# A bidirectional mixer layer on one core: the triangular substitution moved from VectorE to GpSimd, with its transposes placed later

## The chip, the cores and the metric

The kernel runs on 1 core of one Trainium2 chip. The metric is the time on the device of one execution, in microseconds. Before the change three runs took 2184.51, 2187.23 and 2191.09 us, with a median of 2187.23 us.

The engines go by their names in the profile: PE is TensorE (PEld its loading of weights), DVE is VectorE, ACT is ScalarE, POOL is GpSimd, SP is SyncE, which issues the DMAs here. Each engine works through its own queue in order and waits for others by semaphores.

## The reference, cut to what matters

The reference is one encoder layer over a sequence of 1024 positions with 1024 channels. A normalised, modulated input h is projected by w_in to all branches; three branches mix along the sequence (A an mLSTM, B a long convolution, C the RWKV-7 recurrence); their gated outputs are merged and projected. The change lies in branch C, which runs this recurrence in both directions for 16 heads of 64 channels:

```python
def rwkv7_scan(r, w, k, v, kk, a, reverse):
    def step(state, inp):
        r_t, w_t, k_t, v_t, kk_t, a_t = inp
        sa = jnp.einsum('bhij,bhj->bhi', state, -kk_t)
        state = (state * w_t[:, :, None, :] + sa[..., None] * (kk_t * a_t)[:, :, None, :]
                 + v_t[..., None] * k_t[:, :, None, :])
        return state, jnp.einsum('bhij,bhj->bhi', state, r_t)
    xs = tuple(jnp.moveaxis(t.astype(jnp.float32), 1, 0) for t in (r, w, k, v, kk, a))
    _, ys = lax.scan(step, jnp.zeros((B, H, N, N), jnp.float32), xs, reverse=reverse)
    return jnp.moveaxis(ys, 0, 1)
...
proj = h @ w_in[l]
```

The kernel computes it in chunks of 64 positions. Within a chunk each sa depends on those before it, which is a triangular system of 64 x 64 for each head, direction and chunk. The kernel inverts these systems ahead of the scan.

## The kernel before

**Stages.** The kernel normalises the input and forms h (`modulate`), runs branches A and B, then branch C (`rwkv`), then the merge. Beside the branches it works off a list of jobs, which are projections of h by tiles of w_in. One job's tile of weights is loaded in four parts (`load_w`): ScalarE rounds a part to wh (L333), GpSimd makes the rest wl = wraw - wh (L334), and TensorE multiplies three times per 128 channels (L351 to L353). There are four buffers of wh and of wl, as many as one tile has parts, so a part of the next tile is made only when TensorE is through with the same part of the tile before.

**Branch C.** `rwkv` goes over 8 pairs of heads. The scan of a pair (`scan`) has 16 chunks m, each with four yields, so 64 steps. One chunk is a chain: TensorE forms U, VectorE copies it to us (L1769), TensorE multiplies us by the inverse tt to SA, VectorE and ScalarE copy SA into SV (L1775, L1776), TensorE forms SN, VectorE adds the state and scales it (sn, L476), and VectorE and ScalarE copy the result into SV for the next chunk (L1800, L1801). `setup` makes G and B for two chunks at a time.

**What runs beside the scan.** `weave` runs the scan and, at fixed steps, the next piece of other generators: `prep` (the factors ar and bk of a half pair), `load`, `bonus` and `post` (the head's norm and output), and `tphase`. Between the steps it works off the projections (`fill`). The inverses come from `tphase`, in two groups: those of chunks 8 to 15 of a pair (g = 1) while chunks 1 to 6 are scanned, those of chunks 0 to 7 of the next pair (g = 0) while chunks 10 to 15 are scanned. The step tuples of `put` say at which of the 64 steps each piece is issued. The pieces of `tphase` are issued under `ahead(..., TP)`, which raises their priority by 400 instructions.

**One tphase.** TensorE forms the products pq, ScalarE copies them out to quad and q21, VectorE transposes quad into Ab (L1625), and a DMA fills Tb with its initial value (L1628). Then the substitution runs over 31 rows: row l forms a product tm of column l of Ab with row l of Tb (L1633) and adds it into the rows of Tb below (L1636), 62 instructions in all, each dependent on the one before. Both are issued by the helper `tt`, so the profile files them under its line, L476. The rows are issued in pieces of five. Then two transposes on VectorE make t1 (L1641) and t2 (L1644), TensorE multiplies q21 by t1 to pw, ScalarE copies that to W and t2 into tt, TensorE multiplies W by t2 to px, and ScalarE copies px into tt.

**The order on an engine.** A scheduler puts each engine's instructions in order by priority, ahead of the run. `issue_after(x)` lets an instruction come no earlier in that order than x, and `in_turn` keeps groups of products together. On the chip each engine keeps to its order.

Of the kernel before, what the change touches and what calls it, by code (L numbers as in the profile page):

```python
# [23 lines left out]
TP, PP, PW, RA = 400, 0, 3, 2  # L24
# [4 lines left out]
MUL, ADD, SUB, MAX, MIN = ALU.mult, ALU.add, ALU.subtract, ALU.max, ALU.min  # L29
# [16 lines left out]
def run(g):  # L46
    for _ in g:
        pass
# [11 lines left out]
def ahead(tc, gen, by):  # L60

    while True:
        if by:
            with tc.high_priority(by):
                if next(gen, gen) is gen:
                    return
        elif next(gen, gen) is gen:
                return
        yield


def weave(fg, at, fill, per):

    i, owed = 0, 0.0
    for _ in fg:
        for g in at.pop(i, ()):
            next(g, None)
        owed += per
        fill(int(owed))
        owed -= int(owed)  # L80
        i += 1
    for i in sorted(at):
        for g in at[i]:
            next(g, None)
# [201 lines left out]
class Trunk:  # L286
# [1060 lines left out]
    def rwkv(self, yc_out, pairs=range(8)):  # L1347
        nc, tc, A = self.nc, self.tc, self.A
        with ExitStack() as c2:
# [37 lines left out]

            pairs = list(pairs)
            n = len(pairs)
            cx = [dict(p=p, ar={}, al={}, bk={}, pc={}) for p in pairs]  # L1390
            run(self.load(cx[0]))
            for g in range(2):
# [8 lines left out]
            for i in range(n):  # L1401
                at = {}

                def put(gen, *steps):
                    for s in steps:
                        at.setdefault(s, []).append(gen)
                put(prep1, 0, 0, 1, 2, 3, 4, 4)
                put(self.bonus(cx[i]), 5, 6, 7)
                put(ahead(tc, self.tphase(cx[i], 1), TP), *range(6, 28, 2))
                if i + 1 < n:  # L1410
                    nx = cx[i + 1]
                    put(self.load(nx, cx[i - 1] if i else None), 8, 9, 10, 11)
                    put(ahead(tc, self.prep(nx, 0, 0), PP), 15, 16, 19, 33, 33)
                    put(ahead(tc, self.prep(nx, 0, 1), PP), 34, 35, 36, 37, 37)
                    put(ahead(tc, self.tphase(nx, 0), TP), *range(39, 62, 2))
                    prep1 = ahead(tc, chain(self.prep(nx, 1, 0), self.prep(nx, 1, 1)), PP)
                    put(prep1, 40, 42, 49)
                if i > 0:
                    put(self.post(cx[i - 1], yc_out, i + 1 == n), 5, 6, 7, 8, 11, 12, 13, 14)
                weave(self.scan(cx[i], cx[i + 1] if i + 1 < n else None), at, self.fill, max(0, self.left() - 6) / (64.0 * (n - i + 0.1)))  # L1420
# [176 lines left out]
    def tphase(self, cx, g):  # L1597

        nc, rp = self.nc, self.rp
        x2 = lambda n: self.ep.tile([128, 16, 32], F32, name=n, tag="x2", bufs=3)
        q, q21 = x2("quad"), self.ep.tile([128, 16, 32], F32, name="q21", tag="q21", bufs=1)
        pq = [x.rearrange("p (c t) -> p c t", t=CL) for x in self.banks("pq")]
# [19 lines left out]
        Ab = self.ep.tile([128, 32, 32], F32, name="Ab", tag="Ab", bufs=1)  # L1624
        nc.vector.transpose(Ab.rearrange("p t (g u) -> p t g u", g=2),  # L1625
                            q.rearrange("p u t -> p t u").unsqueeze(2).broadcast_to([128, 32, 2, 16]))
        Tb = x2("Tb").rearrange("p a b -> p (a b)").rearrange("p (t s) -> p t s", s=16)
        nc.sync.dma_start(Tb, self.A["tinit"])  # L1628
        tm = rp.tile([128, 136], F32, name="tm", tag="tm", bufs=1)
        for l in range(31):  # L1630
            n, m = 31 - l, l // 2 + 1
            x = tm[:, 0:n * m].rearrange("p (a b) -> p a b", b=m)
            self.tt(x, Ab[:, l + 1:32, l].unsqueeze(2).broadcast_to([128, n, m]),  # L1633
                    Tb[:, l, 0:m].unsqueeze(1).broadcast_to([128, n, m]))
            o = Tb[:, l + 1:32, 0:m]
            self.tt(o, o, x, ADD)  # L1636
            if l % 5 == 4:
                yield
        tt = self.tt_t[g]
        t1 = x2("t1").rearrange("p a b -> p (a b)").rearrange("p (v s) -> p v s", s=16)  # L1640
        nc.vector.transpose(t1.rearrange("p v s -> p s v"), Tb.rearrange("p t s -> p s t"))  # L1641
        t1 = t1.rearrange("p (g u) s -> p u s g", g=2)
        t2 = x2("t2")
        nc.vector.transpose(t2.rearrange("p u (s g) -> p u s g", g=2), t1)  # L1644
# [95 lines left out]
    def scan(self, cx, nx):  # L1740

        nc, rp = self.nc, self.rp
# [11 lines left out]
        for m in range(16):  # L1754
# [4 lines left out]
            if j == 0:  # L1759
                ahead = self.setup(cx, m // 2 + 1) if m < 14 else self.setup(nx, 0) if nx else iter(())  # L1760
            ch = self.ps.tile([128, 4, 2, CL], F32, name="pch", tag="c", bufs=2)
            U, SA, SN, py = (ch[:, i] for i in range(4))
# [3 lines left out]
            if late:  # L1766
                late[0](ins)
            us = self.sm.tile([128, 2, CL], F32, name="us", tag="us", bufs=2)
            nc.vector.tensor_copy(us, U)  # L1769
            ins = self.in_turn(partial(nc.tensor.matmul, SA[hsl[h], d], tt[hsl[h], 8 * d + c, :], us[hsl[h], d],  # L1770
                                       start=True, stop=True) for d in range(2) for h in range(2))
            if late:
# [143 lines left out]
```

## Time and profile before

| | before |
|---|---|
| median of 3 runs | 2187.23 us |
| lowest, highest | 2184.51, 2191.09 us |
| profiled execution, own time | 2200.05 us |
| its span (first to last instruction) | 2198.3 us |
| mean granted TensorE clock | 0.956 |
| first to last copy of us (the scan stage) | 929.5 to 1983.3 us |

The profile is of one execution, which has its own time. A row of the groups of instructions gives the line, the engine, the operation, what it writes and reads, the shapes and how often, then the busy time in all and the mean of one, then the idle time ahead of them and what ended it. A row of the timeline gives the start and the length in us. A row of windows gives a stretch, its length, the busy time of each engine with its count of instructions, the granted clock and the DMA share. A row of the waits names who waited for whom, the sum, the count and the longest. TensorE's matmuls are pipelined, so its busy time contains more than the time in which its array computes.

### The profile page before, as it was taken

To read this page: it belongs to the slowest core of one execution; us is meant where nothing else is said; L and a number is where in the kernel's file an instruction comes from. 1 tells how busy PE (TensorE), PEld (TensorE's weight loads), DVE (VectorE), ACT (ScalarE), POOL (GpSimd) and SP (SyncE) were. 2 spreads that over 40 slices of the span, in tenths; PEclk is the share of its full clock that TensorE was granted. 3 is DMA by queue.
4 is the path that set the end of the run, shared out by engine and by line. 5 is a ranking of instruction groups with operands and counts; after the bars stand their busy time and mean duration, and the time that the engine had idled before them with its cause. 6 is when DMAs were issued, how large, how long until landed. Compare 5 with 4: busy or idle time off the path is not lost. (4 is left out here: it accounts for less than half of the span.)

```text
span 2198.3 us, 45984 instructions
## 1 busy us (share of the span) xinstructions
PE 1994.0 (91%) x17098; PEld 1509.2 (69%) x17098; DVE 1634.6 (74%) x4754; ACT 1103.2 (50%) x2558; POOL 424.3 (19%) x485
## 2 busy tenths in 40 slices
PE   6999899999989899899989999999898887897998
PEld 4666777787868677666766676666666665675786
DVE  4854999988447947788787888868887888764536
ACT  5557356454242115664665756667466564532221
POOL 2211311122222432311101111111114411010200
PEclk9999999999999999999998999999899998897999
DMA  8211222334465345321322333224143542445623
GB/s 255 70 67 59 78 77 90 112 101 127 143 200 172 119 138 163 124 68 61 130 79 93 117 106 102 92 81 136 52 155 118 187 144 63 159 143 175 196 89 129
DMA packets 169384, 262.19 MB, mean 119 GB/s; under 512 B 17863, under 2 KB 87335, under 8 KB 169160
## 3 DMA queue, kind: packets, MB, share of 16 engines
q1 hardware_dynamic: 169160, 259.25, 36.3%
q8 instruction: 135, 2.21, 0.4%
q14 instruction: 89, 0.73, 0.1%
HBM read 181.06 MB, written 78.12 MB: 118 GB/s over the span
## 5 line engine op out<-in xcount | busy, mean ns | idle before, releaser
L334 POOL TENSOR_TENSOR wl<-wraw,wh 128x256 fp32r<-128x256 f32 x408 | 371.5, 915 | 1488.6 <-ACT wh L333 1464.8
L351 PE MATMUL pg<-hh,wh 128*128 128x512 f32 x1440 | 601.5, 418 | 20.9 <-ACT wh L333 11.8
L352 PE MATMUL pg<-hh,wl 128*128 128x512 f32 x1440 | 594.3, 413 | 16.4 <-POOL wl L334 16.3
L353 PE MATMUL pg<-hl,wh 128*128 128x512 f32 x1440 | 592.4, 412 | 1.9 <-DVE hl L565 1.8
L351 PEld LDWEIGHTS pg<-hh,wh 128*128 128x128 f32 x1440 | 278.7, 194 | 88.9 <-ACT wh L333 15.1
L352 PEld LDWEIGHTS pg<-hh,wl 128*128 128x128 f32 x1440 | 279.3, 194 | 78.0 <-POOL wl L334 22.2
L353 PEld LDWEIGHTS pg<-hl,wh 128*128 128x128 f32 x1440 | 278.1, 193 | 62.0 <-DVE hl L565 2.8
L333 ACT CAST wh<-wraw 128x256 fp32r<-128x256 f32 x408 | 162.7, 404 | 220.6 <-PE pg L353 122.1
L476 DVE TENSOR_TENSOR tm<-Ab,Tb 128x126 f32<-128x126 f32 (+22 forms) x496 | 145.4, 293 | 4.4 <-DMA Tb<-in_tinit 2.7
L476 DVE TENSOR_TENSOR Tb<-Tb,tm 128x126 f32<-128x126 f32 (+22 forms) x496 | 144.2, 291 | 1.9
L473 DVE SCALAR_TENSOR_TENSOR st<-pg,hmu,st 128x511 f32<-128x511 f32 (+1 forms) x130 | 80.9, 636 | 27.9 <-ACT e L424 17.6
L476 DVE TENSOR_TENSOR G<-pgr,gmask 128x512 f32<-128x512 f32 x128 | 85.4, 679 | 17.0 <-PE pgr L398 17.0
L457 ACT ACTIVATE st<-pg 128x512 f32<-128x512 f32 x74 | 44.2, 597 | 99.9 <-PE pg L353 95.0
L1684 ACT COPY G<-ar 64x128 f32<-64x128 f32 x256 | 64.3, 295 | 48.4 <-DVE G L476 46.6
L473 DVE SCALAR_TENSOR_TENSOR st<-st,pg 128x512 f32<-128x512 f32 x80 | 54.3, 679 | 35.7 <-PE pg L353 12.7
L398 PE MATMUL pgr<-ar,bk 64*128 64x128 f32 x896 | 76.9, 287 | 0.0
L141 DVE SCALAR_TENSOR_TENSOR row<-row 64x1 f32<-64x1 f32 x393 | 72.7, 208 | 2.1
L1769 DVE COPY us<-pch 128x128 f32<-128x128 f32 x128 | 36.3, 283 | 45.8 <-PE pch L398 45.5
L395 PEld LDWEIGHTS pch<-SV,G 128*64 128x64 f32 x256 | 25.3, 139 | 65.5 <-ACT SV L1801 52.3
L395 PE MATMUL pch<-SV,G 128*64 128x64 f32 x256 | 43.2, 252 | 27.7 <-ACT SV L1801 26.2
L476 DVE TENSOR_TENSOR dw<-dw,dw 128x512 f32<-128x512 f32 x92 | 67.1, 760 | 0.9
L395 PEld LDWEIGHTS pch<-SV,B 128*64 128x64 f32 x256 | 25.3, 139 | 60.1 <-ACT SV L1776 50.1
(677 smaller groups left out, 4228.4 us busy)
## 6 DMA issues: line engine op xcount, KB each, us to landing
wraw<-in_w_in SPq DMA_DIRECT2D x340, 128.0 KB, 2.3
low<-lora SPq DMA_DIRECT2D x32, 512.0 KB, 4.1
sig<-st SPq DMA_DIRECT2D x48, 256.0 KB, 2.6
st<-sig SPq DMA_DIRECT2D x48, 256.0 KB, 3.5
wraw<-in_w_br SPq DMA_DIRECT2D x68, 128.0 KB, 2.8
adw<-in_ada_w SPq DMA_DIRECT2D x16, 512.0 KB, 7.1
x<-in_x SPq DMA_DIRECT2D x8, 512.0 KB, 6.1
hx<-st SPq DMA_DIRECT2D x16, 256.0 KB, 2.0
```

The costliest lines, as they stand in the source:

```text
L141: self.ops.append(lambda: self.nc.vector.scalar_tensor_tensor(o, a, s, b, op0=op0, op1=op1))
L333: self.nc.scalar.copy(hi, raw)
L334: self.nc.gpsimd.tensor_tensor(lo, raw, hi.bitcast(F32), op=SUB)
L351: nc.tensor.matmul(p, wh, hh, start=(k == 0), stop=False)
L352: nc.tensor.matmul(p, wl, hh, start=False, stop=False)
L353: nc.tensor.matmul(p, wh, hl, start=False, stop=(k == n - 1))
L395: ins = f()
L398: ins = f()
L457: self.nc.scalar.activation(o, p, AF.Tanh, scale=0.5)
L473: return self.nc.vector.scalar_tensor_tensor(out, in0, s, in1, op0=op0, op1=op1)
L476: return self.nc.vector.tensor_tensor(out, a, b, op=op)
L1684: nc.scalar.copy(G[0:64, :, d, h, 0:64], cx["al"][g, d, b % 4][hsl[h]])
```

## The change

The 62 instructions of a substitution are issued on GpSimd instead of VectorE. The scan notes its latest copy of us in `self.mark`, and the first transpose (t1) may stand in VectorE's order no earlier than the one that is latest when it is issued. `tphase` has one more yield, between the substitution and the transposes, and the steps at which its pieces are issued change: the substitution's pieces now follow at consecutive steps, and the transposes stand at steps 24 and 57 (before at 20 and 53), the parts behind them at 26, 28 and 59, 61 (before at 22, 24 and 55, 57).

```diff
+            self.mark = None
...
-                put(ahead(tc, self.tphase(cx[i], 1), TP), *range(6, 28, 2))
+                put(ahead(tc, self.tphase(cx[i], 1), TP), 6, *range(7, 14), 24, 26, 28)
...
-                    put(ahead(tc, self.tphase(nx, 0), TP), *range(39, 62, 2))
+                    put(ahead(tc, self.tphase(nx, 0), TP), 39, *range(40, 47), 57, 59, 61)
...
         for l in range(31):
             n, m = 31 - l, l // 2 + 1
             x = tm[:, 0:n * m].rearrange("p (a b) -> p a b", b=m)
-            self.tt(x, Ab[:, l + 1:32, l].unsqueeze(2).broadcast_to([128, n, m]),
-                    Tb[:, l, 0:m].unsqueeze(1).broadcast_to([128, n, m]))
+            nc.gpsimd.tensor_tensor(x, Ab[:, l + 1:32, l].unsqueeze(2).broadcast_to([128, n, m]),
+                                    Tb[:, l, 0:m].unsqueeze(1).broadcast_to([128, n, m]), op=MUL)
             o = Tb[:, l + 1:32, 0:m]
-            self.tt(o, o, x, ADD)
+            nc.gpsimd.tensor_tensor(o, o, x, op=ADD)
             if l % 5 == 4:
                 yield
+        yield
...
-        nc.vector.transpose(t1.rearrange("p v s -> p s v"), Tb.rearrange("p t s -> p s t"))
+
+        with tc.issue_after(self.mark.ins) if self.mark else ExitStack():
+            nc.vector.transpose(t1.rearrange("p v s -> p s v"), Tb.rearrange("p t s -> p s t"))
...
-            nc.vector.tensor_copy(us, U)
+            self.mark = nc.vector.tensor_copy(us, U)
```

VectorE's order at the end of a substitution, in the third pair's scan (group g = 1). Before, the instructions of the substitution alternate with those of the preparation (bk) and of the scan (SV, sn), and the transposes follow the last of them:

```order
L476 TENSOR_TENSOR tm_13040<-Ab_13036,Tb_13038 128x45
L476 TENSOR_TENSOR bk_13704<-a_13248,s_13246 128x4x64
L476 TENSOR_TENSOR Tb_13038<-Tb_13038,tm_13040 128x3x15
L1775 COPY SV_13366<-pch_13498 64x2x64
L476 TENSOR_TENSOR tm_13040<-Ab_13036,Tb_13038 128x30
L476 TENSOR_TENSOR Tb_13038<-Tb_13038,tm_13040 128x2x15
L476 TENSOR_TENSOR tm_13040<-Ab_13036,Tb_13038 128x16
L476 TENSOR_TENSOR Tb_13038<-Tb_13038,tm_13040 128x16
L1641 STREAM_TRANSPOSE t1_13433<-Tb_13038 128x16x32
L476 TENSOR_TENSOR sn_13587<-pch_13498,sn_13447 128x128
L1644 STREAM_TRANSPOSE t2_13435<-t1_13433 128x512
```

The same place with the change (lines are four to five higher; st are projections being finished, ar and bk are the preparation's):

```order
L473 SCALAR_TENSOR_TENSOR st_13666<-pg_13558,hmu_76,st_13666 128x511
L473 SCALAR_TENSOR_TENSOR ar_13703<-kk_13071,P_13269 128x4x64
L476 TENSOR_TENSOR a_13270<-k_13061,a_13270 128x512
L1773 COPY us_13463<-pch_13454 128x128
L1645 STREAM_TRANSPOSE t1_13477<-Tb_13005 128x16x32
L476 TENSOR_TENSOR bk_13374<-a_13270,s_13268 128x4x64
L1648 STREAM_TRANSPOSE t2_13479<-t1_13477 128x512
L1779 COPY SV_13368<-pch_13454 64x2x64
L476 TENSOR_TENSOR G_13493<-pgr_13494,gmask_8471 128x4x128 x2
L473 SCALAR_TENSOR_TENSOR st_13666<-pg_13558,hmu_76,st_13666 128x511
```

The substitution is gone from VectorE's queue, and the first transpose, which waits for GpSimd, stands between the copy of us and the copy into SV of the same chunk.

GpSimd's order at the end of the same substitution. Before, GpSimd had only the splits of weights and some memsets in this stage; with the change it has the whole chain, and here one split of weights (wl) stands inside it and others behind it:

```order
L1634 TENSOR_TENSOR tm_13007<-Ab_13003,Tb_13005 128x70
L1637 TENSOR_TENSOR Tb_13005<-Tb_13005,tm_13007 128x5x14
L334 TENSOR_TENSOR wl_13382<-wraw_13379,wh_13381 128x256
L1634 TENSOR_TENSOR tm_13007<-Ab_13003,Tb_13005 128x56
L1637 TENSOR_TENSOR Tb_13005<-Tb_13005,tm_13007 128x4x14
...
L1634 TENSOR_TENSOR tm_13007<-Ab_13003,Tb_13005 128x16
L1637 TENSOR_TENSOR Tb_13005<-Tb_13005,tm_13007 128x16
L334 TENSOR_TENSOR wl_13388<-wraw_13385,wh_13387 128x256
```

This wl has 54 of the 62 instructions ahead of it. On TensorE its reader stands among the products of chunk 3 of that scan (plw are products of the preparation, pch those of the scan):

```order
L351 MATMUL pg_13403<-hh0_132,wh_13381 128x512
L352 MATMUL pg_13403<-hh0_132,wl_13382 128x512
L353 MATMUL pg_13403<-hl0_133,wh_13381 128x512
...
L1553 MATMUL plw_13274<-low_13272,w2l_13068 128x512
L352 MATMUL pg_13403<-hh2_136,wl_13388 128x512
L395 MATMUL pch_13189<-SV_12817,B_12810 64x64
L398 MATMUL pch_13189<-SV_12817,B_12810 64x64 x3
```

The products of the scan (pch) stand behind the readers of two parts of wl, one of which is made inside and one behind the substitution on GpSimd.

More of the change, by code (lines that the diff above doesn't have):

```diff
@@ L1597, in tphase @@
     def tphase(self, cx, g):
-        nc, rp = self.nc, self.rp
+        nc, tc, rp = self.nc, self.tc, self.rp
         x2 = lambda n: self.ep.tile([128, 16, 32], F32, name=n, tag="x2", bufs=3)
```

## The prediction

> **What bounds the kernel now.** I read the page first. One execution was profiled: its span is 2198.3 us, its own time 2200.05 us, 0.6% above the median of the three runs (2187.23). Differences are worked out inside this execution and then taken off the median.
>
> ```profile
> span 2198.3 us, 45984 instructions
> ...
> PE 1994.0 (91%) x17098; PEld 1509.2 (69%) x17098; DVE 1634.6 (74%) x4754; ACT 1103.2 (50%) x2558; POOL 424.3 (19%) x485
> ...
> DVE  4854999988447947788787888868887888764536
> ...
> PEclk9999999999999999999998999999899998897999
> ```
>
> TensorE is busy for 91% of the span, GpSimd for 19%. As shares of the whole these say little about the change, which touches only the scan stage, from the first scan step to the last. So next I cut that stage by the two VectorE instructions that enclose a substitution: the transpose into Ab (L1625) and the one that reads the finished Tb (L1641). One such stretch, in VectorE's timeline:
>
> ```profile
> 1405.74 1.96 DVE L1625 STREAM_TRANSPOSE Ab<-quad 128x1024 f32<-128x1024 f32 x1
> ...
> 1438.77 0.28 DVE L1769 COPY us<-pch 128x128 f32<-128x128 f32 x1
> ...
> 1442.96 0.27 DVE L1769 COPY us<-pch 128x128 f32<-128x128 f32 x1
> 1444.33 1.08 DVE L1641 STREAM_TRANSPOSE t<-Tb 128x512 f32<-128x512 f32 x1
> ```
>
> The busy times of the whole stage, of this stretch and of the one behind it, by windows:
>
> ```profile
> core 0: us, PE busy (x) PEld busy (x) DVE busy (x) ACT busy (x) POOL busy (x), PEclk, DMA share, GB/s
> 929.50:1984.00 1054.50, 954.91 (x12126) 702.40 (x12128) 843.59 (x2457) 623.27 (x1550) 169.66 (x215) 0.95 0.34 109
> 1405.70:1444.30 38.60, 35.78 (x362) 25.59 (x364) 35.57 (x126) 15.48 (x41) 7.01 (x8) 1.00 0.18 59
> 1444.30:1470.90 26.60, 24.49 (x430) 18.75 (x427) 11.35 (x28) 17.61 (x43) 3.13 (x4) 1.00 0.39 130
> ```
>
> There are fifteen such stretches in the stage (a sixteenth lies ahead of it). The first, the last and their sum:
>
> ```profile
> 944.10:977.90 33.80, 31.90 (x345) 23.13 (x346) 31.06 (x111) 16.89 (x53) 4.36 (x6) 1.00 0.17 52
> ...
> 1895.70:1937.50 41.80, 37.31 (x361) 26.11 (x361) 35.40 (x116) 19.13 (x55) 4.88 (x6) 0.92 0.38 124
> sum 611.00, PE 542.41 PEld 389.91 DVE 556.01 ACT 321.02 POOL 117.09; mean PE 36.16 PEld 25.99 DVE 37.07 ACT 21.40 POOL 7.81
> ```
>
> A stretch lasts 611.0 / 15 = 40.7 us, and VectorE is busy for 37.07 of it (91%), TensorE for 36.16 (89%). In the 443.5 us of the stage outside the stretches VectorE has 843.59 - 556.01 = 287.6 us (65%) and TensorE 954.91 - 542.41 = 412.5 us (93%). So inside the stretches VectorE is the engine that paces, with TensorE close behind; outside it is TensorE. In the waits of that stage TensorE waits for VectorE's part of the scan step and for ScalarE's, which mostly follows VectorE:
>
> ```profile
> PEld pch L395 <- ACT SV L1801: 52.3, 71, 5.8
> ...
> PEld pch L395 <- DVE us L1769: 25.7, 43, 3.0
> ```
>
> **What leaves VectorE.** The page's two groups of the substitution:
>
> ```profile
> L476 DVE TENSOR_TENSOR tm<-Ab,Tb 128x126 f32<-128x126 f32 (+22 forms) x496 | 145.4, 293 | 4.4 <-DMA Tb<-in_tinit 2.7
> L476 DVE TENSOR_TENSOR Tb<-Tb,tm 128x126 f32<-128x126 f32 (+22 forms) x496 | 144.2, 291 | 1.9
> ```
>
> They are 16 substitutions of 62 instructions, (145.4 + 144.2) / 16 = 18.1 us each. All 18.1 us leave VectorE, which keeps 37.1 - 18.1 = 19.0 us of work in a stretch.
>
> **What GpSimd pays.** The trace of before has no such chain on GpSimd, so I price it from its other two-input instructions and from one dependent pair (a memset that waits for the memset ahead):
>
> ```profile
> L334 POOL TENSOR_TENSOR wl<-wraw,wh x173: 715/742/4257, 876.9 to 1957.6; 128x256 fp32r<-128x256 f32 x173
> ```
>
> ```profile
> L930 POOL TENSOR_TENSOR dml<-dw,dmh 128x512 fp32r<-128x512 f32 x4 | 5.0, 1282 | 0.3 <-ACT dmh L929 0.3
> ```
>
> ```profile
> 198.87 0.95 POOL L671 MEMSET rm<- 64x1024 f32 x1
> 199.88 0.11 POOL L672 MEMSET rm<- 64x8 f32 x1
> ```
>
> The step from 256 elements (0.742 us, median) to 512 (1.282 us) is 2.11 ns per element, which leaves 0.202 us at no elements. A dependent instruction starts 0.06 us after the end of the one ahead (199.88 - 199.82). Row l of the substitution handles (31 - l)(l // 2 + 1) elements twice; over 31 rows that is 5712. So the chain takes 62 x 0.262 + 5712 x 0.00211 = 16.2 + 12.1 = 28.3 us. On average about two splits of weights (L334) stand in GpSimd's queue inside the chain: 1.5 us.
>
> The two engines also get in each other's way. Here GpSimd's wl starts while VectorE works on two-input instructions:
>
> ```profile
> 1429.41 1.74 POOL L334 TENSOR_TENSOR wl<-wraw,wh 128x256 fp32r<-128x256 f32 x1 [12.54 <-ACT wh L333]
> ...
> 1431.43 0.27 DVE L476 TENSOR_TENSOR tm<-Ab,Tb 128x120 f32<-128x120 f32 x1
> ...
> 1432.13 0.83 POOL L334 TENSOR_TENSOR wl<-wraw,wh 128x256 fp32r<-128x256 f32 x1 [0.98 <-ACT wh L333]
> 1432.29 0.81 DVE L476 TENSOR_TENSOR tm<-Ab,Tb 128x121 f32<-128x121 f32 x1
> ```
>
> VectorE's product of 121 elements takes 0.81 us beside a wl, where one of 120 took 0.27; a wl takes 1.74 us behind a run of them instead of 0.742. The Trainium skill, page "SBUF — State Buffer", section "SBUF: two separate sides", says that a GpSimd instruction and a VectorE instruction with two SBUF inputs exclude each other for the whole instruction, and the loser waits; these rows agree with it.
>
> The mean of wl in the stage sizes GpSimd's side:
>
> ```profile
> L334 POOL TENSOR_TENSOR wl<-wraw,wh 128x256 fp32r<-128x256 f32 x173 | 154.3, 896 | 783.4 <-ACT wh L333 763.4 <-PE ptv L1693 11.3 <-issue 4.5
> ```
>
> It is 0.154 us over the median. Half of VectorE's work in a stretch (18.1 of 37.1) is the substitution itself and goes, so I take half of this, 0.077 us x 62 = 4.8 us. The bounds are nothing (28.3 + 1.5 = 29.8 us) and every instruction at wl's mean, 62 x 0.896 = 55.6 us. I take 28.3 + 1.5 + 4.8 = **34.6 us**, the value nearest to the small instructions' own rows. VectorE in turn has 21 to 35 instructions with two SBUF inputs left in a stretch and stands behind GpSimd for at most some 0.2 us (the 92 elements of a mean instruction x 2.11 ns) at each: 4 to 7 us on top of its 19.0, well inside the stretch.
>
> **What is late next.** The transposes now stand in VectorE's queue right behind the copy of us of scan step 6 or 14, and everything behind them waits for them. The stretch is then at least Ab (2.0) + chain (34.6) + 0.2 = 36.8 us, against 40.7: GpSimd's chain allows 3.9 us x 15 = 58 us of gain. How far the scan gets in that time stays about the same: by the order, a stretch holds four steps instead of five, but 45 to 67 other VectorE instructions, where it held 41 to 58. I cost that at nothing, since VectorE has room outside (65%); with the cover gone it would be one more step, some 4 us as in 1438.77 to 1442.96.
>
> Holding the transposes back also moves what follows them, 6.5 us long, in the chain of work:
>
> ```profile
> 1444.41 1.01 DVE t L1641
> ...
> 1450.86 0.27 PE pch L395
> ```
>
> That is the transpose, 64 products, ScalarE's copies into tt, and the first product that needs tt. They now stand at steps 26 and 28 of a tt that is read at 32 (or 59 and 61 of 64), one or more scan steps ahead, so I count nothing for them. No DMA is added: Tb's load is issued with the same step as before, one place earlier in the loop.
>
> TensorE is the other limit. Its 954.91 busy us stay. At the 93% that it has outside the stretches the stage would take 954.91 / 0.93 = 1027 us, a gain of 28 us; at the 97% of a stretch with only projections it would take 982 us, a gain of 72:
>
> ```profile
> 500.00:600.00 100.00, 97.25 (x414) 77.33 (x413) 66.45 (x105) 38.14 (x79) 29.08 (x32) 1.00 0.41 134
> ```
>
> The sum: VectorE gives up 18.1 us per half scan, GpSimd's chain lets through 58 us in all, TensorE 28 to 72. I take TensorE at 94%, since the scan's chain of small products remains: 954.91 / 0.94 = 1016, a gain of 38 us, 2198.3 to 2160 in this profile. On the median: 2187 - 38 = **2149 us**. The substitution ahead of the stage (its transposes stand behind 17 other instructions instead of 52) I leave out, as once 5 us either way.
>
> **The rivals.**
>
> *More comes through (2105 us).* GpSimd's instructions never meet VectorE's, the chain takes 29.8 us, a stretch 32.0: 8.7 x 15 = 131 us by VectorE and GpSimd. TensorE cuts it to 72, with a little more where its matrix work slides into the last scan, which by the order now has projections to its end: 82 us. Against it: wl's mean shows that they do meet.
>
> *GpSimd becomes the bound, slower (2235 us).* The point from which it decides is a chain of 40.7 - 2.2 = 38.5 us, (38.5 - 1.5) / 62 = 0.60 us per instruction. Then VectorE stands at the transposes, and us, sn and SV of the next scan step behind them. A second thing hits earlier: GpSimd serves in order, and a wl that stands behind 54 of the 62 instructions comes only when those are done; TensorE, in order too, stands at the L352 that reads it with the scan's products behind it. At 0.65 us per instruction the chain takes 41.8 us, the stretch 44.0: +3.3 x 15 = +50, near 2235. For it: a wl has taken 4.257 us in this stage where VectorE gave no gap, and so far GpSimd was idle nearly always when a wl was due (763 us of waiting for ScalarE's wh in the row above). Against it: my price is 34.6 / 62 = 0.56 us with everything in it, under 0.60, but not by much.
>
> *The two engines hand it back (2190 us).* If all the VectorE work left in a stretch that reads two SBUF tiles, about half of 19.0 us, is added to the chain, it takes 28.3 + 1.5 + 9.5 = 39.3 us, the stretch 41.5, +12 us in all; if only the part that meets GpSimd's 12.1 us of data out of 28.3, it is 4.1 and a gain remains. Between the two nothing changes. The Trainium skill, page "Perfetto Trace Analysis", section "Optimizing Scalar/DVE Operations", warns of just this: moving work between these two might not help, as they share a port.
>
> That the change doesn't do what it says I give no chance: by the order, all 992 instructions leave VectorE's queue.
>
> **How the numbers follow.** Within 0.3% (7 us) this kernel's runs can't be told from no change. Forecast 44%, more comes through 14%, GpSimd the bound 28%, handed back 14%. The forecast and the first rival are faster, 58%; the third counts 12% as no change and 2% as slower. So faster 58%, same 12%, slower 30%. The range takes in TensorE's 72 us with a margin for the last scan (2095) and the slower rival to 0.67 us per instruction (2250).
>
> **What would show it.** Right: VectorE's busy time 280 us lower, up to some 50 us of waiting in it; chains on GpSimd of 33 to 37 us with 0.5 to 0.6 us per instruction; stretches of 37 us; TensorE at 94% in the stage. Wrong: idle VectorE ahead of L1645 that GpSimd's Tb ends, or L352 waiting for wl for more than a few us per stretch (then the slower rival); a stretch as short as 33 us (the first rival); VectorE's two-input instructions at twice their time (the third).

## The result, and the profile after the change

| | before | changed |
|---|---|---|
| median of the runs (4 each) | 2185.87 us | 2327.77 us |
| lowest, highest | 2179.4, 2191.09 us | 2322.71, 2331.3 us |
| span of the profiled execution | 2198.3 us | 2329.5 us |
| mean granted TensorE clock in it | 0.956 | 0.938 |

The changed kernel is slower: 1.0649 times the time of before, 95% interval 1.0613 to 1.0685, or 141.9 us between the medians. The forecast was 2149 us with a range of 2095 to 2250 us.

The page of the changed kernel: span, busy time of each engine, VectorE's busy tenths in 40 slices, and the shares of the chain that ended last.

```profile
span 2329.5 us, 46011 instructions
...
PE 2004.4 (86%) x17098; PEld 1507.3 (65%) x17098; DVE 1457.8 (63%) x3762; ACT 1098.1 (47%) x2556; POOL 821.0 (35%) x1477
...
DVE  4856899976569575456645665556655554555536
...
PE 43%; POOL 21%; DVE 12%; DMA 9%; issue 9%; ACT 7%; SPq 1%; POOLq 0%; DVEq 0%; ACTq 0%
```

VectorE did get free: 176.8 us less busy, and fives and sixes where it had sevens and eights. GpSimd is busy for only 35%, and yet 21% of the chain goes through it. So it isn't short of time; something waits for its turn. The scan stage lasts 1193.2 us from the first copy of us to the last, where it lasted 1053.8: 141 us more in the first halves of the pairs' scans, 2 us less in the second halves. The groups of the pages, before and changed (after the second bar, the idle time ahead and what ended it), and the waits of the changed kernel's scan stage (us in all, times, longest) say who. Before:

```profile
L352 PE MATMUL pg<-hh,wl 128*128 128x512 f32 x1440 | 594.3, 413 | 16.4 <-POOL wl L334 16.3
...
L1769 DVE COPY us<-pch 128x128 f32<-128x128 f32 x128 | 36.3, 283 | 45.8 <-PE pch L398 45.5
```

Changed:

```profile
L352 PE MATMUL pg<-hh,wl 128*128 128x512 f32 x1440 | 603.7, 419 | 144.8 <-POOL wl L334 144.8
...
L1634 POOL TENSOR_TENSOR tm<-Ab,Tb 128x126 f32<-128x126 f32 (+22 forms) x496 | 204.0, 411 | 135.3 <-DVE Ab L1626 43.4
...
L1637 POOL TENSOR_TENSOR Tb<-Tb,tm 128x126 f32<-128x126 f32 (+22 forms) x496 | 214.1, 432 | 37.2
```

```profile
DVE us L1773 <- PE pch L398: 159.2, 72, 18.4
PEld pg L352 <- POOL wl L334: 126.5, 19, 15.5
PE pg L352 <- POOL wl L334: 120.4, 18, 15.2
```

TensorE stood 120.4 us in the stage for wl, the low half of a projection's weights, in 18 waits of up to 15.2 us; the page of before has 16.4 us of idle time ahead of L352 in the whole execution, the page of the change 144.8. VectorE's wait for the scan's products, 159.2 us where it was 45.5, shows the same loss one engine further: those products stand behind L352 in TensorE's queue.

The place that the order of the change showed, the third pair's first half, on the chip. GpSimd's timeline (start, length, instruction, idle time ahead):

```profile
1227.30 0.25 POOL L1634 TENSOR_TENSOR tm<-Ab,Tb 128x31 f32<-128x31 f32 x1 [5.55 <-DVE Ab L1626]
...
1229.45 0.28 POOL L1634 TENSOR_TENSOR tm<-Ab,Tb 128x58 f32<-128x58 f32 x1
1229.81 0.84 POOL L1637 TENSOR_TENSOR Tb<-Tb,tm 128x58 f32<-128x58 f32 x1
...
1256.48 0.72 POOL L334 TENSOR_TENSOR wl<-wraw,wh 128x256 fp32r<-128x256 f32 x1
...
1259.55 0.22 POOL L1637 TENSOR_TENSOR Tb<-Tb,tm 128x16 f32<-128x16 f32 x1
1259.72 2.09 POOL L334 TENSOR_TENSOR wl<-wraw,wh 128x256 fp32r<-128x256 f32 x3
```

TensorE in the same time:

```profile
1245.70 0.39 PE L352 MATMUL pg<-hh,wl 128*128 128x512 f32 x1
...
1257.26 0.80 PE L352 MATMUL pg<-hh,wl 128*128 128x512 f32 x1 [10.72 <-POOL wl L334]
...
1265.99 0.76 PE L1553 MATMUL plw<-low,w2h 128*128 128x512 f32 x1 [5.80 <-DMA low<-lora]
```

And VectorE's copies of us, one for each chunk. From here on a scan step is one chunk, from one copy of us to the next:

```profile
1242.71 0.28 DVE L1773 COPY us<-pch 128x128 f32<-128x128 f32 x1
...
1272.92 0.29 DVE L1773 COPY us<-pch 128x128 f32<-128x128 f32 x1 [2.50 <-PE pch L398]
...
1291.20 1.10 DVE L1645 STREAM_TRANSPOSE t<-Tb 128x512 f32<-128x512 f32 x1
```

The chain runs from 1227.30 to 1259.77, 32.5 us, two us under the price of 34.6. The wl that stands behind 54 of its 62 instructions starts at 1256.48, and TensorE stands for it from 1246.54 to 1257.26. The wait brings a second one: while wl is not made, the buffers of wraw stay taken, SyncE's next load into one stands, and the load of low, behind it in that queue, comes late (5.80 us at L1553). This scan step takes 30.2 us, where the middle one of the 127 takes 8.4. Every pair has one such step of 22 to 30 us, at chunk 3 or 4; before, the longest of all took 18.9. The transposes, for which the hold was made, wait for nothing here: Tb was ready 31 us earlier.

The wait costs TensorE more than its own length. Rows ahead of it and behind it:

```profile
1245.47 0.39 PE L351 MATMUL pg<-hh,wh 128*128 128x512 f32 x1
1245.70 0.39 PE L352 MATMUL pg<-hh,wl 128*128 128x512 f32 x1
...
1257.85 0.63 PE L353 MATMUL pg<-hl,wh 128*128 128x512 f32 x1
1258.28 0.63 PE L351 MATMUL pg<-hh,wh 128*128 128x512 f32 x1
```

Matmuls of one shape follow each other every 0.23 us ahead of the wait and every 0.43 us behind it. The granted clock is 1.00 in the 8 us ahead and 0.71 in the 8 us behind. The profiled execution has twelve waits of over 5 us for wl, the stage's and one ahead of it: in the 8 us behind each of them the clock is 0.50 to 0.78, in the 8 us ahead it is 1.00 for eleven of the twelve.

### The profile page after: what moved, and what is told of

It is laid out like the page before. It is cut to its first block, busy times and chain, and to the rows that moved or that the text cites. A ratio compares the mean times of both kernels' runs of the same rounds, so it can differ in the third digit from the quotient of the medians.

```text
span 2329.5 us, 46011 instructions
## 1 busy us (share of the span) xinstructions
PE 2004.4 (86%) x17098; PEld 1507.3 (65%) x17098; DVE 1457.8 (63%) x3762; ACT 1098.1 (47%) x2556; POOL 821.0 (35%) x1477
## 4 chain that ended last, share of the span: by engine, by line
PE 43%; POOL 21%; DVE 12%; DMA 9%; issue 9%; ACT 7%; SPq 1%; POOLq 0%; DVEq 0%; ACTq 0%
POOL Tb L1637 9%; POOL tm L1634 8%; PE pg L352 8%; PE pg L351 8%; PE pg L353 8%; PE pout L1259 4%; POOL wl L334 3%; PE pch L398 2%; PE pch L395 2%; DMA wraw<-in_w_in 1%; DMA low<-lora 1%; PE pG L953 1%; PE pwx L398 1%; DMA Tb<-in_tinit 1%; DVE st L473 1%
## 5 line engine op out<-in xcount | busy, mean ns | idle before, releaser
L334 POOL TENSOR_TENSOR wl<-wraw,wh 128x256 fp32r<-128x256 f32 x408 | 355.6, 878 | 1083.7 <-ACT wh L333 1047.7
L352 PE MATMUL pg<-hh,wl 128*128 128x512 f32 x1440 | 603.7, 419 | 144.8 <-POOL wl L334 144.8
L351 PE MATMUL pg<-hh,wh 128*128 128x512 f32 x1440 | 612.1, 425 | 21.4 <-ACT wh L333 14.0
L353 PE MATMUL pg<-hl,wh 128*128 128x512 f32 x1440 | 596.7, 415 | 1.9 <-DVE hl L565 1.8
L352 PEld LDWEIGHTS pg<-hh,wl 128*128 128x128 f32 x1440 | 281.6, 196 | 209.5 <-POOL wl L334 155.7
L351 PEld LDWEIGHTS pg<-hh,wh 128*128 128x128 f32 x1440 | 281.3, 195 | 92.1 <-ACT wh L333 18.1
L353 PEld LDWEIGHTS pg<-hl,wh 128*128 128x128 f32 x1440 | 281.7, 196 | 62.4 <-DVE hl L565 2.8
L1634 POOL TENSOR_TENSOR tm<-Ab,Tb 128x126 f32<-128x126 f32 (+22 forms) x496 | 204.0, 411 | 135.3 <-DVE Ab L1626 43.4
L1637 POOL TENSOR_TENSOR Tb<-Tb,tm 128x126 f32<-128x126 f32 (+22 forms) x496 | 214.1, 432 | 37.2
L476 DVE TENSOR_TENSOR sn<-pch,sn 128x128 f32<-128x128 f32 x120 | 34.4, 287 | 119.0 <-PE pch L398 106.5
L1805 ACT COPY SV<-sn 64x128 f32<-64x128 f32 x120 | 35.6, 296 | 81.9 <-DVE sn L476 78.0
L417 ACT ACTIVATE st<-pg,omu 128x512 f32<-128x512 f32 x52 | 35.8, 688 | 72.6 <-PE pg L353 71.6
```

Of the source, the lines that this page charges most:

```text
L334: self.nc.gpsimd.tensor_tensor(lo, raw, hi.bitcast(F32), op=SUB)
L351: nc.tensor.matmul(p, wh, hh, start=(k == 0), stop=False)
L352: nc.tensor.matmul(p, wl, hh, start=False, stop=False)
L353: nc.tensor.matmul(p, wh, hl, start=False, stop=(k == n - 1))
L476: return self.nc.vector.tensor_tensor(out, a, b, op=op)
L1634: nc.gpsimd.tensor_tensor(x, Ab[:, l + 1:32, l].unsqueeze(2).broadcast_to([128, n, m]), Tb[:, l, 0:m].unsqueeze(1).broadcast_to([128, n, m ...
```

## The experiments

Fifteen kernels were run. Two readings stood against each other at first: Q, that the loss is the place of the wl splits in GpSimd's queue, behind the chain; and the forecast's slower rival, that the chain itself is too long. A third question came up with the first run: whether a free VectorE is worth anything. Each ratio is to the kernel before as it was timed beside that run (medians of 2186.03 to 2189.87 us), with the 95% interval behind it.

### The parts of the change, one at a time (e1 to e4)

**e1**: the changed kernel with the wl splits of the stage on VectorE.

```diff
-        self.nc.gpsimd.tensor_tensor(lo, raw, hi.bitcast(F32), op=SUB)
+        self.we.tensor_tensor(lo, raw, hi.bitcast(F32), op=SUB)
...
+                    self.we = self.nc.vector
                     last = self.rwkv(yc)
+                    self.we = self.nc.gpsimd
```

> The changed kernel, with the splits of weights (L334) on VectorE during the scan stage, so that GpSimd has the substitution alone. Queue theory (TensorE waits for splits that stand behind the chain in GpSimd's queue): the 120 us of TensorE's waiting for wl go, the time falls from 2328 to 2170 to 2230 us. Lock theory (the two engines exclude each other at SBUF): the chain and VectorE's two-input work stay, 160 two-input instructions come on top, the time stays at 2300 us or more. Transposes theory (the held back transposes are late): it stays over 2300.

Measured: 2199.37 us, 1.0048 of before (1.0023 to 1.0074). 128.4 of the 141.9 us come back, though every chain instruction is still on GpSimd. Of TensorE's wait for wl, which VectorE now makes, this is left in the stage:

```profile
PE pg L353 <- DVE wl L335: 2.8, 2, 2.2
```

Q holds. What stays is that nothing is gained; the time is still 0.5% over that of before.

**e2**: the same edit in the kernel before, as a control.

> The kernel before with the same move of the splits, the control: 160 instructions of about 0.41 us, 66 us of work on VectorE, which is 91% busy in the stretches. Expected 2195 to 2225 us; what this costs is to be set against e1.

Measured: 2187.28 us, 1.0003 (0.9983 to 1.0024), although VectorE has the wl splits on top. That is less than the 2195 to 2225 us that were expected. The page's groups of the substitution, on VectorE here, show where a part of their price went:

```profile
L477 DVE TENSOR_TENSOR tm<-Ab,Tb 128x126 f32<-128x126 f32 (+22 forms) x496 | 125.0, 252 | 5.9 <-DMA Tb<-in_tinit 4.0
...
L477 DVE TENSOR_TENSOR Tb<-Tb,tm 128x126 f32<-128x126 f32 (+22 forms) x496 | 124.1, 250 | 2.2
```

With no wl on GpSimd beside them, they take 252 and 250 ns in the mean; before they took 293 and 291. Over 992 instructions that is 40 us (289.6 - 249.1) in their rows. VectorE's busy time in all rises by only 9.4 us, to 1644.0 us, so this run doesn't speak against VectorE as the pace.

**e3**: the substitution on GpSimd, but with the steps of before, without the hold and the extra yield.

```diff
-                put(ahead(tc, self.tphase(cx[i], 1), TP), 6, *range(7, 14), 24, 26, 28)
+                put(ahead(tc, self.tphase(cx[i], 1), TP), *range(6, 28, 2))
...
-        with tc.issue_after(self.mark.ins) if self.mark else ExitStack():
-            nc.vector.transpose(t1.rearrange("p v s -> p s v"), Tb.rearrange("p t s -> p s t"))
+        nc.vector.transpose(t1.rearrange("p v s -> p s v"), Tb.rearrange("p t s -> p s t"))
```

> The substitution on GpSimd with the old steps and without the hold: the engine's change alone. Queue theory: TensorE still waits for wl, 2290 to 2350 us. Transposes theory: the loss was the hold's, so at most 2200. If the hold does what it is for, VectorE now stands idle ahead of the transposes for the chain's Tb, and the time is longer than 2328.

Measured: 2409.12 us, 1.1027 (1.099 to 1.1064), 81 us over the changed kernel and above Q's range. Its waits in the stage:

```profile
PE pg L352 <- POOL wl L334: 20.2, 7, 9.0
...
DVE t L1644 <- POOL Tb L1637: 247.6, 14, 20.2
```

Without the hold VectorE stands 247.6 us for Tb, with the scan behind it in its queue, and TensorE's wait for wl is down to 20.2 us: the loss has moved to another queue and grown. The hold, with its later steps, does what it is for.

**e4**: the changed kernel with `nc.gpsimd` put back to `nc.vector` in the two instructions of the substitution, so that the new steps and the hold stand alone.

> The substitution on VectorE with the new steps and the hold: the placing alone. Queue theory: within 30 us of before, 2160 to 2215, as nothing stands ahead of the splits on GpSimd. Transposes theory: 2300 or more.

Measured: 2185.6 us, 0.999 (0.9969 to 1.0011). They cost nothing by themselves.

### What VectorE's work is worth, and TensorE's (e5 to e7)

**e5**: the last 60 of the 62 instructions replaced by memsets on GpSimd.

```diff
+            if l:
+                for _ in range(2):
+                    nc.gpsimd.memset(Tb[:, 2:32, 0:14], 0.0)
...
+                continue
```

> The changed kernel with the last 60 of the 62 substitution instructions on GpSimd replaced by 60 memsets of 30x14 elements of Tb (the substitution is left out; the memsets read nothing). They fill about as much of GpSimd per substitution, but in GpSimd's queue the wl splits now stand between them, behind at most 41 and mostly behind 1 to 20, where they stood behind 40 to 62. Theory Q (the wl splits' place in the queue makes the loss): TensorE's wait at L352 for wl, 120 us in the changed kernel, falls to 20 to 70 us, and the time to 2210 to 2280 us. Theory L (the length of the chain makes the loss, since the transposes stand for its end): still 2300 to 2330 us, with VectorE's transposes standing for Tb.

Measured: 2170.04 us, 0.9938 (0.9916 to 0.996), below what either theory gave. TensorE's wait for wl is 7.1 us in the stage. GpSimd is busy for 848.8 us, more than with the real chain, so its load is not the cost.

**e6**: the kernel before without 60 of the 62 instructions.

```diff
+            if l == 0:
                 self.tt(x, Ab[:, l + 1:32, l].unsqueeze(2).broadcast_to([128, n, m]),
```

> The kernel before, with 60 of the 62 instructions of each substitution left out and nothing put in their place (the substitution is left out): 16 us and more leave VectorE per substitution, 256 us in the stage, and GpSimd gets nothing. It is the most that the change could have brought. Theory V, the forecast's (VectorE paces the stretches, TensorE stands behind it at 89%): 15 stretches go from 40.7 us towards TensorE's 36.2 us of work at about 94%, so 2120 to 2155 us. Theory T (TensorE paces, and VectorE's work lay beside it): 2165 to 2190 us, within about 1% of the kernel before.

Measured: 2118.26 us, 0.9696 (0.9668 to 0.9724). So VectorE's work is worth 68 us, as V has it, even a little more than its range. The page:

```profile
PE 1963.4 (93%) x17098; PEld 1480.5 (70%) x17098; DVE 1450.6 (68%) x3794; ACT 1101.9 (52%) x2558; POOL 411.2 (19%) x485
```

TensorE is at 93% of the span, and in the stage at 94% (935.6 of 999.4 us), which the forecast took as its limit. Some 30 us of the gain lie ahead of the stage: in the two profiled executions the first copy of us comes at 899.9 us instead of 929.5. The stage itself goes from 1053.8 to 999.1 us.

**e7**: the kernel before without seven of eight matmuls of L353 in the projections of the stage.

```diff
-            nc.tensor.matmul(p, wh, hl, start=False, stop=(k == n - 1))
+            if not self.cut or k == n - 1:
+                nc.tensor.matmul(p, wh, hl, start=False, stop=(k == n - 1))
```

> The kernel before, with seven of every eight matmuls of L353 left out of the projections in this stage (the product of the high half of the weights with the low half of the input is left out): about 551 matmuls of 0.421 us, 232 us of TensorE's work, and VectorE keeps all of its own. Theory V (VectorE paces at 37.07 of 40.7 us): at most 54 us go in 15 stretches, so 2130 to 2170 us. Theory T (TensorE paces): most of the 232 us go until the scan's own chain or VectorE stops it, 1970 to 2080 us.

Measured: 2208.59 us, 1.0116 (1.0083 to 1.0149): 550 matmuls of 0.42 us fewer, and slower, outside the ranges of both theories. The same stretch of time in e7, to be set beside the window of before that the prediction shows (0.95 is the clock there):

```profile
929.50:1984.00 1054.50, 879.21 (x11547) 655.20 (x11543) 834.61 (x2436) 610.93 (x1526) 162.04 (x207) 0.86 0.33 107
```

One of the scan's products, which the edit doesn't touch, in the groups of the stage, in e7:

```profile
L400 PE MATMUL pgr<-ar,bk 64*128 64x128 f32 x868 | 84.4, 313 | 0.0
```

and before:

```profile
L398 PE MATMUL pgr<-ar,bk 64*128 64x128 f32 x882 | 75.7, 287 | 0.0
```

The granted clock falls from 0.95 to 0.86 in the stage, and the products that are left get longer (287 to 313 ns). Part of the missing gain is this clock, so e7 bounds no price and doesn't decide between V and T. That VectorE's work counts rests on e6.

### Half of the change (e8 to e10)

**e8** moves only the second halves' substitutions, **e9** only the first halves', each with its own steps; **e10** moves the last 32 instructions of each.

The choice of the engine in e8 and in e10 (e9 has `g == 1`):

```diff
+        e = nc.gpsimd if g == 0 else nc.vector
```

```diff
+            e = nc.vector if l < 15 else nc.gpsimd
```

> The change for half of the substitutions: those of the second halves (and the one ahead of the first pair) run on GpSimd with the hold and the changed steps, those of the first halves stay on VectorE with the steps of before. In GpSimd's queue no wl split stands behind more than 32 substitution instructions, most behind 4 to 16. Theory Q (the loss is the wl splits' place, and it sits in the first halves): the loss goes, and with 8 of 16 substitutions off VectorE up to half of the 68 us that leaving all of them out brought: 2150 to 2190 us, TensorE's wait at L352 for wl under 20 us in the stage. Theory L (a chain of 31 to 34 us on GpSimd is too long for a half): half of the changed kernel's loss stays, 2235 to 2265 us.

> The mirror image: the substitutions of the first halves on GpSimd with the hold and the changed steps, those of the second halves on VectorE as before. Here the wl splits stand behind 52 to 62 substitution instructions in nearly every first half. Theory Q: all of the loss, 8 first halves with 15 us and more of TensorE's wait for wl each, 2280 to 2340 us. Theory L: half of it, 2235 to 2265 us, as in the second halves' run.

> The changed kernel with the first 15 columns of each substitution (30 of the 62 instructions) put back on VectorE; the last 32 instructions run on GpSimd, about 17 us, and the steps and the hold stay. A wl split stands behind at most 32 of them, in some halves still 22 to 32. About 8 us per substitution leave VectorE, half of what the change took. Theory Q with VectorE as the pace: the wait for wl falls under 40 us and up to half of the 68 us is there to gain, so 2150 to 2200 us. Theory L: with a chain of 8 + 17 us the loss goes as well, so the time is the same; the two part on VectorE's wait for Tb, near nothing by Q and by L.

Measured: e8 2219.74 us, 1.0136 (1.0113 to 1.0159); e9 2224.14 us, 1.018 (1.0148 to 1.0211); e10 2227.47 us, 1.0192 (1.0165 to 1.022). None falls where either theory had it. The wait for wl, of e8 and of e9 in turn:

```profile
PE pg L352 <- POOL wl L334: 51.2, 17, 12.3
```

```profile
PE pg L352 <- POOL wl L334: 61.8, 13, 19.6
```

My reading that only the first halves can lose falls, and so does what it stood on, that no wl in e8 is behind more than 32 instructions. TensorE's longest waits for wl there, 12.3, 8.7, 6.5, 5.4 and 4.8 us, lie beside second halves' chains and the one ahead of the stage. GpSimd's timeline has 41, 29, 24, 53 and 14 instructions of the chain between these wl and the wl or the start of the chain ahead of them. So less than half a chain can be too far back. In e10 this wait is down to 26.4 us and the time isn't; its chain has a hand-over between two engines, whose price was not measured apart. That any part of the chain ahead of a wl costs TensorE fits Q; the times of these three stay unexplained beyond that.

### Why e1 gains nothing (e11 to e15)

**e11** is e6 with the wl splits on VectorE; **e12** is e1 with the memsets of e5 for the chain.

> The kernel before without the substitution (60 of its 62 instructions left out) and with the wl splits of the stage on VectorE: e1 without the chain on GpSimd. It asks why e1, with 122 us less on VectorE than before, gained nothing, where leaving the substitution out gained 68 us. Theory W (the wl splits ate it: about 170 of 0.45 us, 75 us on VectorE, and VectorE standing for wh with the scan's work behind): 2165 to 2195 us. Theory C (the chain on GpSimd ate it, by ending late or by slowing VectorE's instructions beside it): 2115 to 2145 us.

> e1 with the last 60 of the 62 substitution instructions replaced by the memsets of e5 (the substitution is left out; the memsets read nothing): GpSimd is taken for about as long per substitution and no wl split stands in its queue. It differs from e1 in that GpSimd reads no operands beside VectorE. If the reading of operands by both engines at a time ate e1's gain: 2130 to 2165 us, with VectorE's own instructions shorter than in e1. If the chain's late end or the wl splits on VectorE did: 2175 to 2205 us, as e1.

Measured: e11 2107.26 us, 0.9627 (0.9599 to 0.9655); e12 2114.39 us, 0.9656 (0.962 to 0.9693). So wl on VectorE ate nothing (e11 is 11 us below e6), and a GpSimd that is taken for 31 to 34 us per substitution (once 40) need not cost much either. Both lie below all the ranges given for them. But e12 is more than e1 without the reading: in VectorE's order the first transpose stands one scan step later in two of the seven second halves, and the second one in three more. That left two causes, the reading of operands or the hold's place.

**e13** moves only the hold: e1 with the last three pieces of the second halves at later steps. **e14** is the same in the changed kernel.

```diff
-                    put(ahead(tc, self.tphase(nx, 0), TP), 39, *range(40, 47), 57, 59, 61)
+                    put(ahead(tc, self.tphase(nx, 0), TP), 39, *range(40, 47), 60, 61, 62)
```

> e1 (the changed kernel with the wl splits of the stage on VectorE) with the last three steps of the second halves' substitutions at 60, 61 and 62 in place of 57, 59 and 61, which puts their transposes behind one more scan step in VectorE's queue; nothing else differs and nothing is left out. Theory H (in e1 the transposes stand at the head of VectorE's queue for the chain's end, with the scan behind them): the wait for Tb, 29 us in six halves of e1, goes with what stands behind it, and the time comes to 2115 to 2160 us, near e12. Theory R (GpSimd and VectorE reading operands at a time eat it): 2175 to 2200 us, as e1.

> The changed kernel with the same later steps for the second halves, the wl splits left on GpSimd; nothing is left out. Theory Q: the wait for wl in the first halves stays at 100 to 140 us and so does most of the loss; VectorE's wait for Tb, 24 us in the changed kernel, goes: 2285 to 2330 us. If the hold's place is what makes the loss of the change: below 2250 us.

Measured: e13 2163.67 us, 0.9886 (0.9863 to 0.9909), faster than before by 25 us and than e1 by 36; slightly over what H gave, and below R. e14 2328.01 us, 1.0654 (1.0619 to 1.0689): in the changed kernel the same step is worth nothing. There VectorE waits only 5.5 us for Tb in the whole stage, in e1 28.9 us in six second halves: where TensorE's wait for wl holds up the scan, Tb is seldom what comes last. VectorE's timeline at the end of the same second half, in e1:

```profile
1287.25 0.29 DVE L1776 COPY us<-pch 128x128 f32<-128x128 f32 x1 [0.54 <-PE pch L399]
...
1292.28 1.05 DVE L1648 STREAM_TRANSPOSE t<-Tb 128x512 f32<-128x512 f32 x1 [4.74 <-POOL Tb L1640]
...
1299.70 0.29 DVE L1776 COPY us<-pch 128x128 f32<-128x128 f32 x1 [3.39 <-PE pch L399]
```

and in e13:

```profile
1287.14 0.29 DVE L1776 COPY us<-pch 128x128 f32<-128x128 f32 x1 [0.54 <-PE pch L399]
...
1291.91 0.29 DVE L1776 COPY us<-pch 128x128 f32<-128x128 f32 x1 [0.58 <-PE pch L399]
1292.38 1.08 DVE L1648 STREAM_TRANSPOSE t<-Tb 128x512 f32<-128x512 f32 x1 [0.18 <-POOL Tb L1640]
```

Tb is ready at the same time in both. In e1 VectorE stands 4.74 us for it, and the scan step behind it takes 12.5 us; in e13 that step is done first, in 4.8 us, and the wait is 0.18 us.

Two scan steps of over 20 us were left in e13. The chain of work through one of them, in order of time:

```profile
1725.61 0.30 POOL Tb L1640
1727.79 1.27 POOL hl L1109
1729.08 0.60 ACT st L469
1730.03 0.41 ACT wh L334
1730.46 0.80 DVE wl L335
```

It is the same thing with another instruction: hl, the low half of the merge's input, stands on GpSimd behind the chain, ScalarE stands for hl, VectorE for ScalarE, TensorE for the scan. **e15** therefore leaves the chain alone on GpSimd: to the edits of e13 it adds these, and the substitution ahead of the stage stays on VectorE.

```diff
-                nc.gpsimd.tensor_tensor(ys[i][1][:, sl], raw, ys[i][0][:, sl].bitcast(F32), op=SUB)
+                self.we.tensor_tensor(ys[i][1][:, sl], raw, ys[i][0][:, sl].bitcast(F32), op=SUB)
...
-        nc.gpsimd.memset(s[:, :, 0:1], 0.0)
+        nc.vector.memset(s[:, :, 0:1], 0.0)
...
+        e = nc.gpsimd if self.mark else nc.vector
...
-                nc.gpsimd.memset(SV[0:64], 0.0)
+                nc.vector.memset(SV[0:64], 0.0)
```

> e13 with everything else of the stage off GpSimd too: the low halves of the merge's input and two memsets go to VectorE, and the first substitution, ahead of the scans, where nothing lies beside it, stays on VectorE. Nothing is left out. Theory Q (whatever stands behind the chain in GpSimd's queue loses): the two scan steps of 23.2 and 20.7 us in e13's last pairs fall to about 10, and TensorE's 16 us of wait ahead of the first pair go: 13 + 10 + 10 us, 2125 to 2145 us. Theory R (what is left comes from operands read by two engines at a time): 2150 to 2170 us, as e13.

Measured: 2144.78 us, 0.9799 (0.9761 to 0.9837), 45 us faster than the kernel before, at the upper end of Q's range. This is the fastest of the kernels that leave nothing out. One long scan step stays, 24.7 us in the last pair: a load into Ab's buffer (for the merge) stands in SyncE's queue until the chain is done with Ab, and a load that VectorE needs stands behind it; VectorE waits 18.6 us for that one.

## Why the prediction was wrong, point by point

- **VectorE paces the stretches: held, as far as e6 shows.** It gained 68 us by VectorE's work alone, in its profile 55 of them in the stage. e7 doesn't speak for it or against it, as its clock was lower.
- **18.1 us leave VectorE per substitution: mis-sized.** 176.8 us left in all, 11.1 per substitution. The mean of a group is the length of a row, and most of VectorE's rows overlap (below). The 280 us named as a sign were the same error.
- **GpSimd's chain, 34.6 us, 0.5 to 0.6 us per instruction: held.** Chains took 31 to 34 us, one 37.1. The slower rival's condition, 0.60 us per instruction, was not met by any of them. In e15, the fastest kernel, two of the 15 chains are beyond it (38.0 and 39.6 us, 0.61 and 0.64 us per instruction).
- **Two wl inside the chain, 1.5 us: this is the step that failed.** It counted what a wl costs the chain and not what the chain costs the wl. The mechanism was named, in the rival "GpSimd becomes the bound" (a wl behind 54 of the 62 instructions, TensorE at L352), but hung on the chain's length: it was given 28%, and its +50 us came from 0.65 us per instruction. The loss needed neither. With the chain near its forecast price a wl stands behind 29 us of it at the place shown (1227.30 to 1256.48); TensorE waits for wl 18 times in the stage, up to 15.2 us and 120.4 us in all, and that is most of the loss: e1 takes only the wl out of the queue, 128.4 of 141.9 us come back, and e2 shows that the same edit alone gains nothing.
- **The sign of being wrong that the text named: it came.** "L352 waiting for wl for more than a few us per stretch" is what the trace shows (120.4 us in 15 stretches). The forecast held the change to be faster with 58% and slower with 30%; the time lies above its range, which ended at 2250 us.
- **What is late next, the hold: too short by one scan step in the second halves.** The text put the transposes behind step 6 or 14 and asked only whether a stretch was long enough. With the wl out of the way e13 shows 36 us for it; in the changed kernel it was worth nothing (e14).
- **TensorE's limit, a gain of 38 us: the right size, and not reached by this change.** e15, with the chain of 15 of the 16 substitutions on GpSimd, gains 45 us and ends at 2144.78 us, where the forecast had 2149. That the two meet is in part luck: e15 is another kernel, and its stage lasts 1013 us with TensorE busy for 934 of them (92%), where the forecast had 1016 us with 955 (94%).
- **The substitution ahead of the stage, 5 us: too small.** With the change the stage begins 11 us sooner (918.4 against 929.5 us), and without the substitution 18 to 30 us sooner (e11 against e2, e6 against before), all in single profiled executions.
- **The engines hand it back: real but not decisive.** The sum of the state, `sn<-sn,pc`, takes 303 ns in the mean without the chain (e11) and 372 ns with it on GpSimd (e1), both with wl on VectorE: not twice its time. Chain instructions of one size differ as much as 0.28 and 0.84 us, as the rows at 1229.45 and 1229.81 show; during the longer one VectorE reads two tiles from SBUF (for hsp, 1229.80 to 1230.48). That agrees with the exclusion that the Trainium skill, page "SBUF — State Buffer", section "SBUF: two separate sides", describes. The Trainium skill, page "Perfetto Trace Analysis", section "Optimizing Scalar/DVE Operations", warned that such a move might not help; e15 shows that here it does, by 2.0% (1.6 to 2.4%), once nothing else stands in GpSimd's queue in the stage. How much of the 30 us between e15 and e12 is the reading of operands by both engines was not isolated: their orders differ as well.

## What to carry to other kernels

When work is moved to an idle engine, look at the short instructions that were already there: the engine serves in order, so each of them now comes as late as the work ahead of it lasts, and what it costs is decided by who waits for them, not by the engine's share of busy time. Price both directions, what they add to the moved work and what it adds to them, by their places in the order. And after one wait is gone, measure again what stands behind it: here the hold, worth nothing in the changed kernel, was worth 36 us once the first queue was clear.

## What the runs showed of the hardware that was not expected

**Rows of VectorE overlap where the next doesn't need the one ahead.** Consecutive rows of VectorE's timeline in the kernel before:

```profile
1413.64 0.23 DVE L476 TENSOR_TENSOR Tb<-Tb,tm 128x81 f32<-128x81 f32 x1
1413.79 0.21 DVE L476 TENSOR_TENSOR y<-y,pch 128x64 f32<-128x64 f32 x1
1413.92 0.23 DVE L476 TENSOR_TENSOR tm<-Ab,Tb 128x78 f32<-128x78 f32 x1
```

Each starts 0.08 us or so before the one ahead ends (1413.64 + 0.23 = 1413.87, the next at 1413.79). Where a row needs the one right ahead of it, there is a gap instead:

```profile
946.06 0.20 DVE L476 TENSOR_TENSOR tm<-Ab,Tb 128x31 f32<-128x31 f32 x1
946.30 0.21 DVE L476 TENSOR_TENSOR Tb<-Tb,tm 128x31 f32<-128x31 f32 x1
```

Here it is 0.04 us (946.06 + 0.20 = 946.26). The chain's instructions on GpSimd, each of which needs the one ahead, have a gap as well: 1229.45 + 0.28 = 1229.73, the next at 1229.81. The wl behind the chain, which doesn't need it, starts at 1259.72, ahead of the end of the last row (1259.55 + 0.22 = 1259.77). So a sum of means overstates what VectorE gives up when other work stands between the rows: 289.6 us by the page's groups, 176.8 us by its busy time, and 184.0 us where 960 of the 992 instructions were left out (e6).

**With less work for TensorE its clock was lower.** With 550 matmuls fewer the granted clock fell from 0.956 to 0.910 over the span and the time rose by 1.2% (e7). Why is not shown. In most of these runs the clock and TensorE's busy share go together (0.981 at 93% in e6, 0.938 at 86% in the changed kernel); e7, with 0.910 at 87%, is lower than that would give. In the changed kernel the clock falls right behind each long wait of TensorE, as shown with the result, so such a wait costs more than its own length.
